# A hybrid decoder block: the attention head norm reads its PSUM bank, key transposes change banks, and the last head's output moves

## The chip, the cores and the metric

The kernel runs on one core of one Trainium2 chip, as one program. The metric is the device time of one execution in microseconds; the time of a kernel is the median of its runs. The profile is of one further execution, with the time of every instruction.

## What is computed

One decoder block on 512 tokens of width 1024, in float32. A normalised input is projected to queries, keys, values, and to the inputs of a state-space branch and of gates. Two branches run on it, differential attention (8 heads) and a Mamba-2 scan; each is projected, multiplied by sigmoid gates and added; an output projection, a residual and a gated MLP follow. The change touches the attention branch alone:

```python
q = rms_norm(q.reshape(b, s, ATTN_HEADS, 2, ATTN_HEAD_DIM), q_norm_g[l]) * scale
k = rms_norm(k.reshape(b, s, ATTN_HEADS, 2, ATTN_HEAD_DIM), k_norm_g[l])
...
p = jax.nn.softmax(logits, axis=-1)
a = p[:, :, 0] - lam * p[:, :, 1]
return jnp.einsum('bhqk,bhkv->bhqv', a.astype(v.dtype), v)
...
o = rms_norm(o, attn_subln_g[l], SUBLN_EPS) * (1.0 - lam_init)
y_attn = jnp.transpose(o, (0, 2, 1, 3)).reshape(b, s, V_COLS)
```

So each head gives 512 x 128 values `o`, and each row of `o` is scaled by the reciprocal root of its mean square: the head norm.

## The kernel before, in words

Every matrix product is made of three float32r matmuls (high part by high, high by low, low by high), so TensorE does most of the work. Weights arrive in tiles of 128 x 1024 on the SP queue and are split into `wh` (ScalarE, L83) and `wl` (VectorE, L85).

The order of the stages is: input norm, the state-space branch with its projections, attention, the merge of the branches (L775 to L787), the output projection, the MLP. The attention stage is one hand-written list of `pieces`, short runs of projection matmuls that keep TensorE busy: the query, key and value projections of four pairs of heads (`pair_pieces`, 24 pieces of 12 matmuls of 256 columns a pair), gate projections (`gate_pieces`), and at the end part of the projection of the attention output (`pa_pieces`, L709 to L723; the last three pieces have three matmuls each). Between pieces stand the steps of attention, hung on piece numbers by `put`. `steps[n]` is the piece behind which step n stands. With four query tiles of 128 tokens a head, step n does the logits of tile n (`logits`), the transposes of the probabilities of tile n - 2 (`flip_a`), the value matmuls of tile n - 3 (`values`), and in every fourth step `head_out` of a finished head. `prep(h)` transposes the queries and keys of head h five or six pieces ahead of its first logits, for the first head four ahead.

The framework orders each engine's instructions from this order of calls and from when it reckons their inputs to be ready, so an instruction can stand later than it is called. It adds the waits. An engine carries out its instructions in that order.

What the change touches:

- `prep` (L608 to L633): four transposes of queries into one `tp` bank and four of keys into another (L614). ScalarE copies the queries twice (L622, L623), VectorE takes their low part `ql` (L624); the keys are scaled (L629) and their low part taken (L630), `ks`. `tp` has two banks, which `flip_a` (L672) and `head_out` (L701) use as well. `mm`, with three banks, is that of the projections.
- Ahead of it, POOL scales the queries and then the keys of a pair (L586, `qk`).
- `values` (L676 to L696): the value matmuls of a tile go to columns of the one `po` bank (L682). After the fourth tile ScalarE copies the bank to `o` (L689) and squares the four tiles with a row sum each (L691). VectorE turns the sums into scales (L692, `rsqrt` at L113 to L122, L695), 13 small operations, and POOL multiplies `o` by them (L696).
- `head_out` (L698 to L705): four transposes of `o` (L701), then the high and low part `yaH`, `yaL` (L703, L704) for the output projection (L720 to L722, L779 to L781).
- The queue of steps (L744 to L767), where the last head's `head_out` comes behind all pieces.

Of the kernel before, what the change touches and what calls it, by code (L numbers as in the profile page):

```python
# [9 lines left out]
F32 = mybir.dt.float32  # L10
F32R = mybir.dt.float32r
I32 = mybir.dt.int32
AF = mybir.ActivationFunctionType
# [5 lines left out]
P = 128  # L19
S = 512  # L20
# [5 lines left out]
NH = 8  # L26
# [69 lines left out]
def block_kernel(ctx, tc, xt, ws, cols, heads, lams, relb, ident_d, ut_d, onehot_d, mline_d, out):  # L96
    nc = tc.nc
    V, A, G, T = nc.vector, nc.scalar, nc.gpsimd, nc.tensor

    const = ctx.enter_context(tc.tile_pool(name="const", bufs=1))  # L100
    small = ctx.enter_context(tc.tile_pool(name="small", bufs=4))
    dram = ctx.enter_context(tc.tile_pool(name="scratch", bufs=1, space=DRAM))
    mm = ctx.enter_context(tc.tile_pool(name="mm", bufs=3, space=PSUM))
    tpp = ctx.enter_context(tc.tile_pool(name="tpp", bufs=2, space=PSUM))
# [8 lines left out]
    def rsqrt(v, out_t, n, scale=None):  # L113
        it = small.tile([P, 32], I32, name="rsi", bufs=2)[:, :n]
        y = small.tile([P, 32], F32, name="rsy", bufs=2)[:, :n]
        t = small.tile([P, 32], F32, name="rst", bufs=4)[:, :n]
        V.tensor_scalar(out=it, in0=v.bitcast(I32), scalar1=1, scalar2=None, op0=ALU.logical_shift_right)
        V.tensor_scalar(out=y.bitcast(I32), in0=it, scalar1=-1, scalar2=0x5F3759DF, op0=ALU.mult, op1=ALU.add)
        for step in range(3):
            V.scalar_tensor_tensor(out=t, in0=y, scalar=-0.5, in1=y, op0=ALU.mult, op1=ALU.mult)  # L120
            V.tensor_mul(out=t, in0=t, in1=v)
            V.scalar_tensor_tensor(out=out_t if step == 2 else y, in0=t, scalar=1.5, in1=y, op0=ALU.add, op1=ALU.mult)  # L122
# [97 lines left out]
    with tc.tile_pool(name="dtp", bufs=1, side="right", reuse_waits="tile") as dp:  # L220
# [20 lines left out]
        for g in range(NG):  # L241
            nc.sync.dma_start(out=cum_d[g].rearrange("c h l -> h c l"),
                              in_=cum[g * HPG:(g + 1) * HPG, :].rearrange("h (c l) -> h c l", c=NCH))
# [7 lines left out]
        for i, src in enumerate((cum, wrow, dtr)):  # L251
            for c in range(NCH):
                o = (i * NCH + c) * 32
# [229 lines left out]
    for g, (dec0, xw0, chunks, last, norm) in enumerate(SSD_AT):  # L483
        def put(n, f, *a):
            at.setdefault(n, []).append(lambda: f(*a))
# [35 lines left out]
    ap = att_ctx.enter_context(tc.tile_pool(name="att", bufs=2, side="right", reuse_waits="tile"))  # L521
# [86 lines left out]
    def prep(h):  # L608
        st, hh, H = pairs[h // 2], h % 2, heads_[h]
        tps = []  # L610
        for nm in ("q", "k"):
            tp = tpp.tile([P, S], F32, name="tp")
            for t in range(4):
                T.transpose(out=tp[:, t * P:(t + 1) * P],  # L614
                            in_=st[nm][:, t, 2 * hh:2 * hh + 2, :].rearrange("p a d -> p (a d)"), identity=ident)
            tps.append(tp)
        tq, tk = tps
        H["q"], H["k"] = [], []
        for m in range(2):
            a, b = slice(m * 64, m * 64 + 64), slice(64 - m * 64, 128 - m * 64)  # L620
            q2 = ap.tile([P, S], F32R, name=f"qq{m}")
            A.copy(out=q2[a], in_=tq[a])  # L622
            A.copy(out=q2[b], in_=tq[a])  # L623
            V.tensor_sub(out=qlow[hh][m][a], in0=tq[a], in1=q2[a].bitcast(F32))  # L624
            H["q"].append(q2)
        for m in range(2):
            a, b = slice(m * 64, m * 64 + 64), slice(64 - m * 64, 128 - m * 64)
            k2 = ap.tile([P, S], F32R, name=f"ks{m}")
            A.activation(out=k2[a], in_=tk[a], func=AF.Copy, scale=gqk[a, 0:1])  # L629
            V.scalar_tensor_tensor(out=k2[b], in0=tk[a], scalar=gqk[a, 0:1], in1=k2[a].bitcast(F32),  # L630
                                   op0=ALU.mult, op1=ALU.subtract)
            H["k"].append(k2)
        H["r"] = small.tile([P, 4, 2], F32, name="es", bufs=3)  # L633
# [42 lines left out]
    def values(h, i):  # L676
        H, hh, vt = heads_[h], h % 2, pairs[h // 2]["v"]
        if i == 0:
            H["po"] = pop.tile([P, S], F32, name="po")
        po, aT = H["po"], H["aT", i]  # L680
        for b in range(i + 1):
            T.matmul(po[:, i * P:(i + 1) * P], lhsT=aT[:, b * P:(b + 1) * P], rhs=vt[:, b, hh * P:(hh + 1) * P],  # L682
                     start=(b == 0), stop=(b == i))
        if i < 3:
            return
        o = H["o"] = ap.tile([P, 4, P], F32, name="o")
        sq = ap.tile([P, P], F32, name="qksq", bufs=1)
        v = small.tile([P, 4], F32, name="ov", bufs=3)
        A.copy(out=o.rearrange("p a d -> p (a d)"), in_=po)  # L689
        for t in range(4):  # L690
            A.activation(out=sq, in_=o[:, t], func=AF.Square, scale=H["r"][:, t, 0:1], accum_out=v[:, t:t + 1])  # L691
        V.tensor_scalar(out=v, in0=v, scalar1=1.0 / P, scalar2=1e-5, op0=ALU.mult, op1=ALU.add)  # L692
        rr = small.tile([P, 4], F32, name="orr", bufs=2)
        rsqrt(v, rr, 4)
        V.scalar_tensor_tensor(out=rr, in0=rr, scalar=1.0 - LAM_INIT, in1=H["r"][:, :, 0], op0=ALU.mult, op1=ALU.mult)  # L695
        G.tensor_mul(out=o, in0=o, in1=rr.unsqueeze(2).to_broadcast([P, 4, P]))  # L696

    def head_out(h):  # L698
        tp = tpp.tile([P, S], F32, name="tp")
# [30 lines left out]
    pieces, start, todo = pair_pieces(0), [], {}  # L730
# [13 lines left out]
    steps = []  # L744
    for p_ in range(4):
        steps += [start[p_] + n for n in ((0, 3, 7, 10, 14, 17, 21, 24) if p_ < 2 else range(0, 24, 3))]
    steps += [steps[-1] + n for n in (3, 6, 9, 12, 15)]
    put(0, load_bias, 0)
    put(4, load_bias, 1)
    for h in range(NH):  # L750
        first = steps[4 * h] if h else start[0] + 1
        put(first - 6 if h % 2 else first - 5, prep, h)
    for n in range(4 * NH + 5):
        for f, back in ((logits, 0), (flip_a, 2), (values, 3)):
            if 0 <= n - back < 4 * NH:
                put(steps[n], f, (n - back) // 4, (n - back) % 4)
        if n % 4 == 3 and n // 4 + 2 < NH:
            put(steps[n], load_bias, n // 4 + 2)
        if n >= 8 and n % 4 == 0:
            put(steps[n], head_out, n // 4 - 2)  # L760
    for n, f in enumerate(pieces):
        f()
        for g in todo.pop(n, []):
            g()
# [35 lines left out]
    with tc.tile_pool(name="rsp", bufs=2, space=PSUM, reuse_waits="tile") as rsp, tc.tile_pool(name="wo", bufs=2, side="right", reuse_waits="tile") as op:  # L800
# [21 lines left out]
        first = []  # L822
# [136 lines left out]
```

## Time and profile before

| | |
|---|---|
| median of 3 runs | 1152.47 us (1152.27, 1152.47, 1157.36) |
| the profiled execution | 1156.34 us, span 1154.4 us |
| TensorE matmul | 1122.7 us busy, 97% of the span |
| VectorE | 760.8 us, 66% |
| ScalarE | 580.8 us, 50% |
| POOL | 121.7 us, 11% |
| granted TensorE clock | 0.995 of full speed over the span |

Times in the trace are microseconds from the start of the span. A wait is idle time of an engine ahead of an instruction, and the releaser named beside it is the instruction whose end it waited for. The attention stage lies between about 440 and 715 us. Matmuls overlap: each lasts longer than the distance to the next, so the rate of TensorE is read from starts.

### The profile page before, as it was taken

The page shows a single profiled execution, that of the slowest core. Times are in us where ns is not written, and L with a number is a line of the kernel's source. Part 1 is how long each engine was busy: PE and PEld are TensorE (multiplying, and loading weights), DVE is VectorE, ACT ScalarE, POOL GpSimd, SP SyncE. Part 2 cuts the span into 40 slices and gives each one's busy share as a digit, 9 for nine tenths or more (in the row PEclk, how much of TensorE's full clock was granted, in tenths as well). Part 3 has the DMA queues.
Part 4 walks back from the last instruction along what each step waited for, and adds up shares of the span by engine and source line. Part 5 has one row for each costly group of instructions (what it writes and reads, how often), then busy time and mean ns, then how long its engine had stood idle before and what let it go on. Part 6 is the DMA issues. An engine that isn't in the chain of part 4 may idle for free. (4 is left out here: it accounts for less than half of the span.)

```text
span 1154.4 us, 15737 instructions
## 1 busy us (share of the span) xinstructions
PE 1122.7 (97%) x5934; PEld 946.7 (82%) x5934; DVE 760.8 (66%) x1280; ACT 580.8 (50%) x1122; POOL 121.7 (11%) x157
## 2 busy tenths in 40 slices
PE   7999999999999999999999998999999999999998
PEld 4778788888887889998988887888888888888887
DVE  6858878669777574577778773646777777772220
ACT  5675665756664232567677663344444444441120
POOL 1002223111222200110101000021000000000000
PEclk9999999999999999999999998999999999999999
DMA  6462434333433223221212120353323333323320
GB/s 230 128 115 91 129 100 136 102 104 112 131 116 102 74 92 106 74 79 60 79 62 77 55 74 27 122 171 91 102 92 109 92 91 104 97 92 116 122 92 19
DMA packets 56556, 114.46 MB, mean 99 GB/s; under 512 B 20816, under 2 KB 28928, under 8 KB 56480
## 3 DMA queue, kind: packets, MB, share of 16 engines
q1 hardware_dynamic: 56336, 113.32, 31.9%
q8 instruction: 47, 0.77, 0.3%
q14 instruction: 29, 0.24, 0.1%
q10 hardware_dynamic: 144, 0.13, 0.0%
HBM read 111.19 MB, written 2.24 MB: 98 GB/s over the span
## 5 line engine op out<-in xcount | busy, mean ns | idle before, releaser
L83 ACT CAST wh<-wr 128x1024 fp32r<-128x1024 f32 x179 | 187.3, 1048 | 217.7 <-PE mm L205 172.9
L85 DVE TENSOR_TENSOR wl<-wr,wh 128x1024 fp32r<-128x1024 f32 x179 | 220.4, 1232 | 114.8 <-ACT wh L83 112.6
L204 PE MATMUL mm<-xH,wh 128*128 128x512 f32 x392 | 157.0, 400 | 8.4 <-ACT xH L176 7.1
L205 PE MATMUL mm<-xL,wh 128*128 128x512 f32 x392 | 155.4, 396 | 0.1
L206 PE MATMUL mm<-xH,wl 128*128 128x512 f32 x392 | 154.5, 394 | 0.0
L206 PE MATMUL mm<-hH,wl 128*128 128x512 f32 x352 | 137.2, 390 | 0.0
L204 PE MATMUL mm<-hH,wh 128*128 128x512 f32 x352 | 137.1, 390 | 0.0
L205 PE MATMUL mm<-hL,wh 128*128 128x512 f32 x352 | 137.1, 389 | 0.0
L538 PE MATMUL mm<-wh,xH 128*128 128x256 f32 x384 | 111.0, 289 | 0.0
L540 PE MATMUL mm<-wh,xL 128*128 128x256 f32 x384 | 109.0, 284 | 0.0
L539 PE MATMUL mm<-wl,xH 128*128 128x256 f32 x384 | 108.7, 283 | 0.0
L204 PEld LDWEIGHTS mm<-xH,wh 128*128 128x128 f32 x392 | 74.6, 190 | 26.6 <-ACT xH L176 7.8
L205 PEld LDWEIGHTS mm<-xL,wh 128*128 128x128 f32 x392 | 74.4, 190 | 16.7 <-DVE xL L177 2.1
L206 PEld LDWEIGHTS mm<-xH,wl 128*128 128x128 f32 x392 | 74.5, 190 | 15.2
L205 PEld LDWEIGHTS mm<-hL,wh 128*128 128x128 f32 x352 | 66.1, 188 | 13.8
L206 PEld LDWEIGHTS mm<-hH,wl 128*128 128x128 f32 x352 | 66.1, 188 | 13.7
L204 PEld LDWEIGHTS mm<-hH,wh 128*128 128x128 f32 x352 | 66.1, 188 | 13.5
L538 PEld LDWEIGHTS mm<-wh,xH 128*128 128x128 f32 x384 | 73.6, 192 | 0.2
L539 PEld LDWEIGHTS mm<-wl,xH 128*128 128x128 f32 x384 | 73.6, 192 | 0.2
L540 PEld LDWEIGHTS mm<-wh,xL 128*128 128x128 f32 x384 | 73.6, 192 | 0.0
L204 PE MATMUL mm<-aH,wh 128*128 128x512 f32 x176 | 68.5, 389 | 0.0
L206 PE MATMUL mm<-aH,wl 128*128 128x512 f32 x176 | 68.5, 389 | 0.0
(239 smaller groups left out, 2174.6 us busy)
## 6 DMA issues: line engine op xcount, KB each, us to landing
wr<-in_ws SPq DMA_DIRECT2D x179, 512.0 KB, 3.5
dec<-cum_d SPq DMA_DIRECT2D x16, 512.0 KB, 5.0
ec<-ecum_d SPq DMA_DIRECT2D x24, 128.0 KB, 4.9
xr<-in_xt SPq DMA_DIRECT2D x8, 256.0 KB, 2.7
out_y<-x SPq DMA_DIRECT2D x7, 256.0 KB, 2.0
x<-in_xt SPq DMA_DIRECT2D x3, 512.0 KB, 6.9
b<-line_d SPq DMA_DIRECT2D x8, 128.0 KB, 2.8
x<-in_xt SPq DMA_DIRECT2D x2, 256.0 KB, 5.2
```

The lines of the kernel that those rows point to most:

```text
L83: nc.scalar.copy(out=hi, in_=raw)
L85: nc.vector.tensor_sub(out=lo, in0=raw, in1=hi.bitcast(F32))
L204: T.matmul(ps, lhsT=h, rhs=rH(k), start=(k == 0), stop=False)
L205: T.matmul(ps, lhsT=h, rhs=rL(k), start=False, stop=False)
L206: T.matmul(ps, lhsT=l, rhs=rH(k), start=False, stop=(k == n - 1))
L538: T.matmul(ps, lhsT=xH[k][:, sl], rhs=h, start=(k == 0), stop=False)
L539: T.matmul(ps, lhsT=xH[k][:, sl], rhs=l, start=False, stop=False)
L540: T.matmul(ps, lhsT=xL[k][:, sl], rhs=h, start=False, stop=(k == NK - 1))
```

## The change

Three things are changed. In `prep` the key transposes go to a bank of `mm` in place of `tp`. In `values` a square with its row sum follows each query tile's value matmuls, straight from the `po` bank; the copy to `o` goes, and the final multiply is made by VectorE from `po`, in place of POOL from `o`. In the queue of steps the first two steps move back by two pieces and one, `prep` of the first head moves back by two pieces, and the last head's `head_out` moves from a step behind all pieces to the step before, which has two pieces behind it.

```diff
-            tp = tpp.tile([P, S], F32, name="tp")
+            tp = tpp.tile([P, S], F32, name="tp") if nm == "q" else mm.tile([P, S], F32, name="mm")
...
+        if i == 0:
+            H["ov"] = small.tile([P, 4], F32, name="ov", bufs=3)
+        v = H["ov"]
+        sq = ap.tile([P, P], F32, name="qksq", bufs=1)
+        A.activation(out=sq, in_=po[:, i * P:(i + 1) * P], func=AF.Square, scale=H["r"][:, i, 0:1], accum_out=v[:, i:i + 1])
         if i < 3:
             return
         o = H["o"] = ap.tile([P, 4, P], F32, name="o")
-        sq = ap.tile([P, P], F32, name="qksq", bufs=1)
-        v = small.tile([P, 4], F32, name="ov", bufs=3)
-        A.copy(out=o.rearrange("p a d -> p (a d)"), in_=po)
-        for t in range(4):
-            A.activation(out=sq, in_=o[:, t], func=AF.Square, scale=H["r"][:, t, 0:1], accum_out=v[:, t:t + 1])
...
-        G.tensor_mul(out=o, in0=o, in1=rr.unsqueeze(2).to_broadcast([P, 4, P]))
+        V.tensor_mul(out=o, in0=po.rearrange("p (a d) -> p a d", a=4), in1=rr.unsqueeze(2).to_broadcast([P, 4, P]))
...
-    steps += [steps[-1] + n for n in (3, 6, 9, 12, 15)]
+    steps[0] += 2
+    steps[1] += 1
+    steps += [steps[-1] + n for n in (3, 6, 9, 12)]
...
-        first = steps[4 * h] if h else start[0] + 1
-        put(first - 6 if h % 2 else first - 5, prep, h)
-    for n in range(4 * NH + 5):
+        put(steps[4 * h] - (6 if h % 2 else 5) if h else start[0] - 2, prep, h)
+    for n in range(4 * NH + 4):
...
+    put(steps[-1], head_out, NH - 1)
```

## Rows read from the trace of the kernel before

**Rows 1.** The page: busy us of each engine, share of the span, instructions.

```profile
PE 1122.7 (97%) x5934; PEld 946.7 (82%) x5934; DVE 760.8 (66%) x1280; ACT 580.8 (50%) x1122; POOL 121.7 (11%) x157
```

**Rows 2.** Waits of PE, 440 to 720 us: in total, times, longest.

```profile
PE tp L701 <- POOL o L696: 9.0, 7, 1.9
PE tp L614 <- POOL qk L586: 2.8, 3, 1.2
PE tp L672 <- DVE ql L624: 1.6, 5, 0.5
```

**Rows 3.** Timeline of PE, head 0: start, us, instruction [idle before <-releaser].

```profile
519.06 1.05 PE L682 MATMUL po<-vt,aT 128*128 128x128 f32 x8
...
525.99 0.38 PE L682 MATMUL po<-vt,aT 128*128 128x128 f32 x2
...
533.54 0.36 PE L538 MATMUL mm<-wh,xH 128*128 128x256 f32 x1
...
535.30 0.28 PE L540 MATMUL mm<-wh,xL 128*128 128x256 f32 x1
536.72 0.65 PE L701 MATMUL tp<-ident,o 128*128 128x128 f32 x4 [1.14 <-POOL o L696]
```

**Rows 4.** Timeline of ACT, head 0: the copy of the bank.

```profile
520.15 0.59 ACT L689 COPY o<-po 128x512 f32<-128x512 f32 x1 [0.57 <-PE po L682]
```

**Rows 5.** Timeline of DVE, 519 to 537 us.

```profile
521.90 0.17 DVE L662 RECIPROCAL es<-sums 128x2 f32<-128x2 f32 x1 [1.40 <-ACT p L660]
...
526.17 0.17 DVE L692 TENSOR_SCALAR ov<-ov 128x4 f32<-128x4 f32 x1
...
535.33 0.15 DVE L695 SCALAR_TENSOR_TENSOR orr<-orr,es 128x4 f32<-128x4 f32 x1
```

**Rows 6.** Timelines of ACT, DVE and POOL, the last head's norm.

```profile
705.95 0.59 ACT L689 COPY o<-po 128x512 f32<-128x512 f32 x1 [5.07 <-PE po L682]
...
708.46 0.19 ACT L691 ACTIVATION_READ_ACCUMULATOR qksq<-o,es 128x1 f32 x1
...
708.68 0.17 DVE L692 TENSOR_SCALAR ov<-ov 128x4 f32<-128x4 f32 x1 [10.37 <-ACT qksq L691]
...
711.14 0.16 DVE L695 SCALAR_TENSOR_TENSOR orr<-orr,es 128x4 f32<-128x4 f32 x1
...
711.47 1.04 POOL L696 TENSOR_TENSOR o<-o,orr 128x512 f32<-128x512 f32 x1 [15.38 <-DVE orr L695]
```

**Rows 7.** Timeline of PE at the end of the attention stage.

```profile
705.62 0.48 PE L720 MATMUL mm<-yaH,wh 128*128 128x512 f32 x1
...
710.25 0.39 PE L722 MATMUL mm<-yaH,wl 128*128 128x512 f32 x1
712.56 0.75 PE L701 MATMUL tp<-ident,o 128*128 128x128 f32 x4 [1.93 <-POOL o L696]
714.08 1.65 PE L779 MATMUL mm<-yaH,wh 128*128 128x512 f32 x3 [0.78 <-ACT yaH L703]
```

**Rows 8.** Windows: us, busy (x) PE PEld DVE ACT POOL, PEclk, DMA share, GB/s.

```profile
525.00:550.00 25.00, 23.63 (x177) 22.12 (x176) 18.41 (x46) 16.75 (x40) 1.45 (x2) 1.00 0.24 72
...
714.10:719.80 5.70, 5.70 (x14) 4.46 (x14) 3.73 (x5) 2.94 (x3) 0.00 (x0) 0.50 0.00 0
```

**Rows 9.** Groups by line, DVE, 480 to 712 us: busy, mean ns, idle before.

```profile
L558 DVE TENSOR_TENSOR gt<-mm,r_bc 128x512 f32<-128x512 f32 x8 | 5.5, 688 | 2.8 <-PE mm L556 2.8
```

**Rows 10.** Timelines of PE and POOL, the first head's transposes.

```profile
472.45 0.66 PE L614 MATMUL tp<-ident,qk 128*128 128x128 f32 x4 [0.56 <-POOL qk L586]
474.31 0.65 PE L614 MATMUL tp<-ident,qk 128*128 128x128 f32 x4 [1.20 <-POOL qk L586]
...
470.49 3.76 POOL L586 TENSOR_TENSOR qk<-qk,qkr 128x1024 f32<-128x1024 f32 x2 [21.83 <-PE mm L540]
```

**Rows 11.** Timelines of DVE and PE, head 5: last key read, next projection.

```profile
609.67 0.76 DVE L630 SCALAR_TENSOR_TENSOR ks<-tp,gqk,ks 64x512 fp32r<-64x512 f32 x1
...
610.69 0.36 PE L538 MATMUL mm<-wh,xH 128*128 128x256 f32 x1
```

## The prediction

> **What bounds the kernel now.** First the busy line of the page [rows 1]: TensorE (PE) is busy 97% of the span, VectorE (DVE) 66%, ScalarE (ACT) 50%, GpSimd (POOL) 11%. The change adds and removes no matmul, so all it can give back is time in which PE stands still or runs slowly. Second, the waits of PE in the attention stretch, 440 to 720 us [rows 2]: 9.0 us at L701, the transposes of a finished head, waiting for POOL's scaling at L696; 2.8 us at L614, the transposes of queries and keys; 1.6 us at L672, waiting for a PSUM bank that the query copies of `prep` still read. With the 0.78 us at the first L779 [rows 7] these 14.2 us, and what the clock does behind them, are the whole stake. The ends of matmuls are modelled, so a wait may cost some 0.1 us more than its row says.
>
> Third, why the head is late. The eight value matmuls of head 0 begin at 519.06 and last 1.05 us [rows 3]. ACT copies the bank at 520.15 [rows 4], but with other ACT work between its four squares the small rsqrt operations on DVE only begin at 526.17, and they run until 535.48 [rows 5], where the same 13 operations with DVE to themselves, in the last head, take from 708.68 to 711.30 [rows 6]. POOL scales for 1.04 us, and PE starts the transposes at 536.72 after 1.14 us of standing still [rows 3]. L701 is called directly behind the value matmuls of its step, yet 15 projection matmuls, issued from 533.54 to 535.30, stand between them on PE: the order of issue already allows for a late head, just not late enough.
>
> Fourth, the end of the stage, where nothing is left to fill PE [rows 6, 7]: last matmul of the pieces issued at 710.25, transposes at 712.56, first L779 at 714.08, and then matmuls that take twice their time. In 714.10 to 719.80 the granted clock is 0.50, that is 1.2 of 2.4 GHz, after PE had done only four transposes between 710.6 and 714.1 [rows 7, 8].
>
> **The change, part by part.**
>
> *Heads 0 to 6.* The copy of 128x512 (0.59 us, ACT) and the scaling on POOL (1.04 us) go; the four squares stay, but three run one, two and three steps earlier, each as its columns arrive. Behind the last value matmul stand one square, the 13 small DVE operations and a DVE multiply. A square costs (708.65 - 706.54) / 4 = 0.53 us with its accumulator read [rows 6]; from PSUM I take the same (0.2 us more or less would change nothing below). The multiply reads PSUM, as L558 does: 0.69 us [rows 9]. So head 0's chain begins at 520.11 + 0.04 + 0.53 = 520.7 instead of 526.2. Undisturbed it ends 2.62 + 0.69 us later, at 524.0; stretched to 9.3 us as now, at 530.7. Both lie before 535.4, where PE wants the result. The wait at L701 should vanish: 9.0 - 1.93 (last head) = **7.1 us** gained.
>
> What hides the new work: 8 x 0.69 = 5.5 us are added to DVE and 8 x 0.59 = 4.7 us taken from ACT over some 235 us; DVE waits between operations there (1.40 us at 521.90, just where the chain moves to [rows 5]). Without that cover the cost would be at most 5.5 us. Each early square waits on ACT for PE, with exponentials, copies and weight casts queued behind it; head 0's copy waited for PE in the same way and began 0.04 us after the last value matmul [rows 3, 4], so I take nothing for it. If the next value matmuls must wait for a square in the same bank, they have a step of 6.9 us (519.06 to 525.99) for 0.6 us of work.
>
> A sentence of the Trainium skill speaks against this part: VectorE: DVE Perf Modes, section "Rules for kernel authors", says to copy PSUM to SBUF first if many operations follow. The trace does not show that a copy would pay: the multiply that reads PSUM takes 0.69 us, and the copy alone 0.59 [rows 4, 9]; by the rule ACT would keep 4.7 us of copies, which PE does not see.
>
> *The wait that takes its place.* The single `po` bank was free when the copy ended, at 520.74. Now it is held until the multiply ends, and the next head's first value matmuls want it at 525.99 [rows 3]. Between 524.0 and 530.7 lies that time, so each of seven heads costs between nothing and 4.7 us. I take 0.3 us each, **-2 us**: the chain starts where DVE has gaps, and the issue order was seen above to push waiting PE work back, so only what it misjudges is lost.
>
> *Last head.* Square from 705.95 to 706.5, chain 2.62 us, multiply 0.69 us: ready at 709.8 instead of 712.51. `head_out` now stands behind piece 33, with two pieces, six matmuls, left. The 21 matmuls from 705.62 to 710.25 are (710.25 - 705.62) / 20 = 0.23 us apart [rows 7], so the first 15 end at 709.1; transposes from 709.85 to 710.5; six matmuls to 711.9, which cover the 0.69 us eviction; L779 at 711.9 instead of 714.08: **2.2 us**. PE then stands still 0.75 us at most, shorter than the 1.14 us at head 0, around which the granted clock stays at 1.00 [rows 8]. So the clock should stay up: 14 matmuls took 5.70 us instead of 14 x 0.23 = 3.2, **2.5 us** [rows 8]. The moved step issues four transposes, one ACT and one DVE operation, no DMA.
>
> *First head.* `prep(0)` stands two pieces later (2 x 12 matmuls of 256 columns, at (535.30 - 533.54) / 14 = 0.13 us [rows 3], some 3 us). Now its query transposes wait 0.56 us, its key transposes 1.20 us for POOL, which ends at 474.25 [rows 10]. With 3 us more work ahead of them both inputs are there: **1.8 us**. The logits of the first two tiles move back by two and one pieces, so `prep` keeps its lead; no DMA moves past another queue. The third L614 wait (2.8 - 1.8 = 1.0 us) stays.
>
> *Key transposes in a projection bank.* With the keys elsewhere a second `tp` bank is free for the transposes of probabilities: the 1.6 us of L672 [rows 2] should go, **1.6 us**. In return one of three `mm` banks is held until the last read of the keys. In the tightest place I found, in head 5, the keys are read until 610.43, and a projection starts at 610.69 [rows 11]: nearly even. Bounds 0 and 3 us for all heads; I take **-1 us**.
>
> *Sum.* 7.1 + 2.2 + 2.5 + 1.8 + 1.6 - 2 - 1 = 12.2 us against the profiled execution of 1156.34 us (span 1154.4): 1144.1. That execution lies 3.9 us above the median of 1152.47. Whether the median runs lost 2.5 us at the clock too is not shown; without it they gain 9.7 (1142.8), with it 12.2 (1140.3). I take **1142.0 us**.
>
> **The rivals.**
>
> *The stall only moves.* PE waits at L682 for the multiply instead of at L701 for POOL, about as long per head, and the 7.1 us are not gained: 1142 + 7 = 1149 us. For it: the chain's stretch on DVE, 9.3 against 2.6 us, is the same kind of misjudged lateness. Against it: the chain starts earlier. The Trainium skill, PSUM — Partial Sum Buffer, section "Summary: rules for kernel authors", says to evacuate PSUM promptly, and this change does the opposite; no row of before shows a PE wait on `po`. Chance 0.16.
>
> *The `po` bank becomes the bound (slower).* Place: L682 of the next head's first tile. It decides once the chain behind the last square takes over 525.99 - 520.7 - 0.69 = 4.6 us and PE's order is not pushed back. Price 4.7 us in seven heads, 33 us, against 14.2 gained: 1142 + 31 = 1173 us; half of it 1157 to 1158. For it: the chain takes 9.3 us now. Against it: those are 9.3 us amid the next head's query and key operations, and three squares no longer stand in front. Chance 0.06.
>
> *The heads stay late, or `mm` banks run short.* The multiply is placed so late on DVE that L701 still waits, or five heads each pay 1 to 2 us for a projection bank: 1147 to 1149 us. For it: head 5 above. Against it: 4.7 us between 530.7 and 535.4. Chance 0.14.
>
> **How the numbers follow.** The forecast has 0.64: 1137 (the new waits at zero, somewhat more than the rows at each stall) to 1146.7. Half a per cent of the median is 5.8 us, about what a measurement of this kernel can tell from no change, so faster is below 1146.7: 0.64 and a third of the 1147 to 1149 cases, 0.74. Within: 0.20. Slower: 0.06. The range from 1137 to 1150.5 leaves out the slow rival and a little at both ends.
>
> **What would show it.** Right: no L701 wait on POOL in heads 0 to 6; the small DVE chain beginning within about 1 us of the last value matmul; no stretch at granted clock 0.50 near 712; L614 waits down to about 1 us; L672 no longer waiting on `ql`. Wrong: waits of PE at L682 on the DVE multiply of more than 1 us a head, or of the projections (L538, L554) on `ks`, or PE's still time in 440 to 720 above 8 us.

## The result and the profile after

The changed kernel takes 1142.18 us in the median of four runs (1140.65 to 1143.94), the kernel before 1152.68 in the median of four beside it. The ratio is 0.990, with a 95% interval of 0.987 to 0.993: faster, 10.5 us, where 1142.0 was forecast. The profiled execution took 1140.65 us, span 1138.8 us.

The busy line of the page of the kernel after, which answers to [rows 1]:

```profile
PE 1116.3 (98%) x5934; PEld 943.0 (83%) x5934; DVE 766.3 (67%) x1288; ACT 574.6 (50%) x1114; POOL 110.0 (10%) x149
```

VectorE has 5.5 us more to do, ScalarE 6.2 and POOL 11.7 us less. Where the time came from is read stretch by stretch. In the windows below the columns are those of [rows 8]; the first stretch runs from the first query projection to the first matmul of the merge, the second to the last matmul of the merge. First the kernel before, then the kernel after:

```profile
441.50:714.10 272.60, 258.01 (x1873) 240.55 (x1871) 181.60 (x467) 167.16 (x409) 28.55 (x24) 1.00 0.22 69
714.10:745.50 31.40, 31.40 (x127) 25.71 (x128) 22.09 (x29) 11.46 (x14) 0.00 (x0) 0.91 0.34 106
```

```profile
439.20:700.80 261.60, 257.13 (x1872) 241.22 (x1871) 186.69 (x475) 160.94 (x401) 18.61 (x16) 1.00 0.24 72
700.80:729.60 28.80, 28.80 (x128) 23.52 (x127) 21.82 (x29) 11.45 (x14) 0.00 (x0) 1.00 0.36 116
```

The attention stage is 11.0 us shorter and the merge 2.6 us, the latter at a mean granted clock of 1.00 instead of 0.91. Another 2.3 us of the 15.6 us between these two spans lie ahead of the stage, where both kernels carry out the same instructions: there the profile of before shows a mean granted clock of 0.72 from 76 to 82 us and that of after 1.00. Seven of the twelve profiles taken in all have that stretch, four of them with the new head norm and three without, so it is not counted for the change. What it is worth of the 2.3 us is open: the stage begins between 439.4 and 441.5 us in the profiles with it and between 439.0 and 440.6 us in those without.

The waits of PE, 430 to 715 us, of the kernel after, against [rows 2]:

```profile
PE mm L614 <- POOL qk L586: 1.1, 1, 1.1
PE po L682 <- DVE o L696: 1.1, 4, 0.5
PE mm L538 <- ACT vt L591: 0.9, 1, 0.9
PE lg L649 <- ACT p L660: 0.8, 1, 0.8
PE tp L701 <- DVE o L696: 0.4, 1, 0.4
```

The 9.0 us at L701 have become 0.4, in the last head alone; L672 waits for nothing. What is new is small: 1.1 us for the `po` bank (the rows of the weight loads show more of it, see the last run below), 0.9 us of a projection that waits for a bank near 478 us, and 0.5 us more at the logits.

Head 0, timeline of DVE and then of PE, of the kernel after, against [rows 3, 5]:

```profile
516.67 0.17 DVE L692 TENSOR_SCALAR ov<-ov 128x4 f32<-128x4 f32 x1 [0.20 <-ACT qksq L688]
...
519.01 1.22 DVE L85 TENSOR_TENSOR wl<-wr,wh 128x1024 fp32r<-128x1024 f32 x1
...
520.41 1.23 DVE L85 TENSOR_TENSOR wl<-wr,wh 128x1024 fp32r<-128x1024 f32 x1
521.56 0.16 DVE L695 SCALAR_TENSOR_TENSOR orr<-orr,es 128x4 f32<-128x4 f32 x1
521.75 0.69 DVE L696 TENSOR_TENSOR o<-po,orr 128x512 f32<-128x512 f32 x1
```

```profile
515.03 1.05 PE L682 MATMUL po<-vt,aT 128*128 128x128 f32 x8
...
522.50 0.49 PE L682 MATMUL po<-vt,aT 128*128 128x128 f32 x2 [0.15 <-DVE o L696]
...
529.56 0.60 PE L701 MATMUL tp<-ident,o 128*128 128x128 f32 x4
```

The small chain begins 0.59 us after the last value matmul (516.08), not 6.1 us, and takes 5.05 us with two weight splits in between. The multiply ends at 522.44, and 0.06 us later the next head's first value matmuls enter the bank: they now follow the multiply closely. The head's transposes come 7.1 us after it and wait for nothing.

The end of the stage, timeline of PE of the kernel after, against [rows 7]:

```profile
694.15 1.05 PE L682 MATMUL po<-vt,aT 128*128 128x128 f32 x8
...
698.45 0.39 PE L720 MATMUL mm<-yaH,wh 128*128 128x512 f32 x1
699.20 0.63 PE L701 MATMUL tp<-ident,o 128*128 128x128 f32 x4 [0.36 <-DVE o L696]
...
700.83 0.86 PE L781 MATMUL mm<-yaH,wh 128*128 128x512 f32 x3
```

From the end of the last value matmuls to the first matmul of the merge 700.83 - 695.20 = 5.6 us pass. Before, those value matmuls stood at

```profile
704.81 1.05 PE L682 MATMUL po<-vt,aT 128*128 128x128 f32 x8
```

and it was 714.08 - 705.86 = 8.2 us.

### The profile page after: what moved, and what is told of

The parts are those of the page before. It is cut to its first block, busy times and chain, and to the rows that moved or that the text cites. A ratio compares the mean times of both kernels' runs of the same rounds, so it can differ in the third digit from the quotient of the medians.

```text
span 1138.8 us, 15720 instructions
## 1 busy us (share of the span) xinstructions
PE 1116.3 (98%) x5934; PEld 943.0 (83%) x5934; DVE 766.3 (67%) x1288; ACT 574.6 (50%) x1114; POOL 110.0 (10%) x149
## 4 chain that ended last, share of the span: by engine, by line
PE 86%; DVE 6%; ACT 3%; DMA 2%; issue 1%; SPq 1%; POOL 0%; DVEq 0%; ACTq 0%
PE mm L204 20%; PE mm L206 20%; PE mm L205 20%; PE mm L538 3%; PE mm L540 3%; PE mm L539 3%; DVE wl L85 1%; PE po L682 1%; PE sm L445 1%; ACT wh L83 1%; PE mm L555 1%; PE mm L554 1%; PE mm L556 1%; SPq L387 1%; PE sm L422 1%
## 5 line engine op out<-in xcount | busy, mean ns | idle before, releaser
L205 PE MATMUL mm<-aL,wh 128*128 128x512 f32 x176 | 68.5, 389 | 0.0
```

The source lines that it names most:

```text
L205: T.matmul(ps, lhsT=h, rhs=rL(k), start=False, stop=False)
```

## The experiments

The theory was the prediction's: late heads cost some 7 us at their transposes, the end of the stage the rest, and the parts add up. The first run repeats the kernel before, the next three are the parts alone.

**The kernel before once more**, unchanged, for the clock term.

> The kernel before, unchanged, profiled a second time. The profiled execution behind the prediction took 1156.34 us and showed the granted clock at 0.50 for about 7 us behind the last head and for about 3 us near 78 us. Theory A (the clock falls in nearly every execution of before): the new profile shows the stretch behind the last head again, and a time of 1152 to 1157. Rival B (the clock falls only in the slow-lying executions of before, so the median of 1152.7 never paid for it): a profile near 1152.5 us has no stretch at 0.50 between 700 and 720 us.

Ratio 1.000 (0.999 to 1.001). The windows of this second profile of before (the first two are stretches at the low clock, the last is the merge):

```profile
472.70:476.10 3.40, 3.40 (x16) 3.40 (x17) 1.78 (x3) 2.20 (x4) 0.00 (x0) 0.50 0.00 0
715.05:718.45 3.40, 3.40 (x10) 2.62 (x9) 2.62 (x4) 2.94 (x3) 0.00 (x0) 0.50 0.03 5
713.90:744.30 30.40, 30.39 (x126) 24.82 (x127) 22.11 (x29) 11.45 (x14) 0.00 (x0) 0.94 0.33 109
```

The clock falls behind the last head again, but for half as long, and the merge takes 30.4 us, 1.0 less than in the first profile and 1.6 more than after. Here it also falls behind the two waits at the first head's transposes. So Theory A holds for whether in the profiles, not for how much: the loss behind the last head is between 1.6 and 2.6 us in these two. In the profiles of the next kernels that keep the old norm the merge takes 30.1 and 30.3 us.

The mean granted clock, which is listed for every execution, says how common this is. Of 54 executions of the kernel before that were listed with it, 11 show 1.000; a stretch of 3.4 us at 0.50 alone would lower the mean to 0.9985 (an estimate from the windows above), so these 11 had none. Their median is 1151.88 us, that of all 54 is 1153.77, and that of the 11 at 0.995, like the profiled one, 1155.64. So "nearly every execution" was too strong. Rival B does not hold as it stands either: 27 of the 54 are at 0.997 or less, so the median pays for the clock somewhere in the span; where, the list does not say.

**The head norm alone.**

```diff
+        sq = ap.tile([P, P], F32, name="qksq", bufs=1)
+        A.activation(out=sq, in_=po[:, i * P:(i + 1) * P], func=AF.Square, ...)
         if i < 3:
             return
...
+        V.tensor_mul(out=o, in0=po.rearrange("p (a d) -> p a d", a=4), ...)
```

> Only the head norm is changed (squares per tile from PSUM, multiply on VectorE from PSUM). Theory A (the head norm is the main part, 7.1 us of waits at the heads' transposes plus most of the end of the stage): 1142 to 1146 us, no wait of PE at the heads' transposes in heads 0 to 6, waits on the po bank of about 1 us in all. Rival (the head norm only pays together with the free tp bank from the key transposes): 1149 to 1153 us.

1145.80 us, ratio 0.993 (0.992 to 0.994), 8.2 us of the runs' 1154.19. Its waits of PE, 430 to 730 us, and its clock at the end of the stage:

```profile
PE tp L614 <- POOL qk L586: 2.9, 3, 1.2
PE tp L672 <- DVE ql L624: 1.9, 3, 1.0
PE po L682 <- DVE o L696: 1.0, 3, 0.4
PE mm L779 <- ACT yaH L703: 0.8, 1, 0.8
PE lg L649 <- ACT p L660: 0.4, 1, 0.4
```

```profile
700.00:712.00 12.00, 11.22 (x50) 8.71 (x49) 8.30 (x21) 3.91 (x6) 0.00 (x0) 1.00 0.07 25
```

No head waits at L701, not even the last, and the clock stays at 1.00 although L779 still waits 0.8 us. The rival, that the norm needs the free bank, falls. The end of the stage on PE:

```profile
698.67 1.05 PE L682 MATMUL po<-vt,aT 128*128 128x128 f32 x8
...
705.72 0.97 PE L779 MATMUL mm<-yaH,wh 128*128 128x512 f32 x3 [0.78 <-ACT yaH L703]
```

From the end of the last value matmuls to the first matmul of the merge 6.0 us pass here, against 8.2 before.

**The key transposes alone.**

```diff
-            tp = tpp.tile([P, S], F32, name="tp")
+            tp = tpp.tile([P, S], F32, name="tp") if nm == "q" else mm.tile([P, S], F32, name="mm")
```

> Only the key transposes go to a projection bank. Theory A: the 1.6 us at the transposes of the probabilities go, about 1 us comes back as waits of projections for a bank: 1151.5 to 1153 us, no change that can be measured. Rival (the shared tp banks delayed whole steps): 1148 to 1150 us. Other rival (projections run short of banks): above 1155 us.

1153.61 us, ratio 1.000 (0.999 to 1.001): no change that can be measured. Its waits of PE, 430 to 730 us:

```profile
PE tp L701 <- POOL o L696: 9.9, 7, 1.9
...
PE lg L649 <- ACT p L660: 1.3, 2, 0.7
```

The 1.6 us at L672 are gone, but 0.9 us more stand at L701 and 1.0 us more at the logits. A theory of mine was wrong in the detail: what comes back is not a wait for a projection bank.

**The first head alone.**

```diff
+    steps[0] += 2
+    steps[1] += 1
...
-        first = steps[4 * h] if h else start[0] + 1
-        put(first - 6 if h % 2 else first - 5, prep, h)
+        put(steps[4 * h] - (6 if h % 2 else 5) if h else start[0] - 2, prep, h)
```

> Only the first head's transposes and the first two steps move back. Theory A: the two waits of 0.56 and 1.20 us at the first head's transposes go: 1150.5 to 1152 us. Rival (the logits of the first head then come late and give it back): 1152.5 us or more, with a new wait of PE before 500 us.

1151.26 us, ratio 0.998 (0.997 to 0.999), 2.4 us of 1154.19. Of its waits the row that mattered:

```profile
PE tp L614 <- POOL qk L586: 1.1, 1, 1.1
```

Of three waits at L614 (2.8 us) the one of head 6 is left, and nothing new stands before 500 us. The gain is a little over the 1.8 us of the two waits; the second profile of before shows the clock at 0.50 just behind them, which may be the rest.

The three parts sum to 8.2 + 0 + 2.4 = 10.6 us, and the whole gave 10.5 us, and 12.3 us in a second comparison (next but one). Within the intervals, some 3 us wide for each part, the parts add up.

**The last head's output, not moved.** Alone, on the kernel before, the moved step was not run. The last head's `o` is ready at 712.51 us there, after the last matmul of the pieces at 710.25 [rows 6, 7], so it should change nothing; that is argued and not shown. With the norm changed it moves four transposes by five matmuls:

```diff
-    steps += [steps[-1] + n for n in (3, 6, 9, 12)]
+    steps += [steps[-1] + n for n in (3, 6, 9, 12, 15)]
...
-    put(steps[-1], head_out, NH - 1)
```

> The changed kernel with the last head's output left behind all pieces, as before. On TensorE this moves four transposes five matmuls later and nothing else. Theory A (the early norm brings the end of the stage, the moved step only its last half microsecond): 0 to 1 us above the changed kernel, a wait of about 0.8 us at the merge's first matmul in place of the 0.36 us at the transposes, granted clock 1.00 throughout. Rival (the moved step is what keeps the clock up): a stretch at 0.50 near 702 us and 2 us or more above the changed kernel.

1141.88 us, ratio 0.990 (0.988 to 0.992), the same as the changed kernel. The wait at the merge and the clock there:

```profile
PE mm L781 <- ACT yaH L703: 0.8, 1, 0.8
```

```profile
698.00:710.00 12.00, 11.22 (x51) 8.75 (x50) 8.76 (x19) 4.29 (x6) 0.00 (x0) 1.00 0.20 66
```

The clock stays up without the moved step; the stage of this run is 262.0 us long against 261.6, in both profiles of the changed kernel. The moved step is worth these 0.4 us by the stage; the medians can't tell it from nothing.

**The changed kernel once more**, beside three variants of it on one chip.

> The changed kernel once more, beside the variants of it. Both theories: 0.988 to 0.992 of before; no stretch at granted clock 0.50 between 690 and 720 us.

1141.16 us, ratio 0.9895 (0.9875 to 0.9914). Its waits are those of the first profile but for the `po` bank, 0.8 us in two heads against 1.1 in four.

**Late squares: the rival of the `po` bank, made worse.**

```diff
-        if i == 0:
-            H["ov"] = small.tile([P, 4], F32, name="ov", bufs=3)
...
-        A.activation(out=sq, in_=po[:, i * P:(i + 1) * P], func=AF.Square, ...)
         if i < 3:
             return
+        v = small.tile([P, 4], F32, name="ov", bufs=3)
...
+        for t in range(4):
+            A.activation(out=sq, in_=po[:, t * P:(t + 1) * P], func=AF.Square, ...)
```

> The changed kernel, but with all four squares behind the last value matmul, from PSUM; the multiply stays on VectorE and the po bank is held some 5 us longer. Theory A (the issue order pushes the next head's value matmuls back, so a longer hold costs only what the order misjudges; what pays is the early start of the small chain): 1 to 5 us above the changed kernel, waits of PE on the po bank of under 1 us a head, and the last head's clock stretch comes back. Rival (the po bank bounds the heads): 14 us or more above the changed kernel, over 2 us of wait at each head's first value matmul.

1144.24 us, ratio 0.992 (0.990 to 0.993), 3.1 us above the changed kernel. Head 0 on DVE and PE, and the waits of PE, 430 to 730 us:

```profile
521.87 0.16 DVE L691 TENSOR_SCALAR ov<-ov 128x4 f32<-128x4 f32 x1
530.41 0.16 DVE L694 SCALAR_TENSOR_TENSOR orr<-orr,es 128x4 f32<-128x4 f32 x1
530.82 0.68 DVE L695 TENSOR_TENSOR o<-po,orr 128x512 f32<-128x512 f32 x1
```

```profile
531.55 0.94 PE L682 MATMUL po<-vt,aT 128*128 128x128 f32 x6 [0.81 <-DVE o L695]
```

```profile
PE po L682 <- DVE o L695: 3.4, 6, 0.8
PE lg L649 <- ACT p L660: 1.4, 2, 0.9
```

The bank is held 9 us longer than in the changed kernel (531.50 against 522.44), and yet the next head's first value matmuls wait 0.81 us: they stand so much later on PE, six in a row, the second tile behind the first. The bank as a bound falls, at 3.4 us where 14 or more were asked. One half of Theory A fell too: with waits of 0.6 and 0.8 us at the end of the stage the clock stayed at 1.00. And that the early start is what pays does not follow from this run: without it the kernel still gains 9.3 us of the 12.3 (some 2.4 of them in the first head), and only the last head waits at its transposes (0.6 us). Head 0's result comes 15.2 us behind its last value matmul, against 16.6 before and 6.4 in the changed kernel.

**Copy and POOL.** Early squares, but the bank is copied and POOL multiplies, as before.

```diff
+        A.copy(out=o.rearrange("p a d -> p (a d)"), in_=po)
...
-        V.tensor_mul(out=o, in0=po.rearrange("p (a d) -> p a d", a=4), ...)
+        G.tensor_mul(out=o, in0=o, ...)
```

> The changed kernel, but ScalarE copies the po bank to SBUF after the fourth square and POOL multiplies the copy, as before the change. Theory A (what pays is the early start, not the engine of the multiply): within 2 us of the changed kernel, no wait on the po bank, at most small waits at the heads' transposes. Rival (POOL's multiply was what made the heads late): the waits of 1.1 to 1.6 us at the heads' transposes are back, 6 to 8 us above the changed kernel.

1140.65 us, ratio 0.989 (0.987 to 0.991), not to be told from the changed kernel. Its wait at the heads' transposes, 430 to 730 us:

```profile
PE tp L702 <- POOL o L697: 2.8, 3, 1.1
```

Three heads wait, up to 1.1 us; four of the seven that waited before do not, though POOL multiplies all of them. No value matmul waits for the bank. So the early start is enough by itself. With the run before, where late squares and the multiply from the bank kept 9.3 us, this says that either half of the new norm takes most of the gain, and that both together take no more than the early start alone. Late squares with the copy kept and the multiply on VectorE were not run, so what in that other half pays, the copy that is gone or the engine, is not shown.

**The two waits that are left.** The first head's keys back in `tp`, head 6 one piece later.

```diff
-            tp = tpp.tile([P, S], F32, name="tp") if nm == "q" else mm.tile(...)
+            tp = tpp.tile([P, S], F32, name="tp") if nm == "q" or h == 0 else mm.tile(...)
...
-        put(steps[4 * h] - (6 if h % 2 else 5) if h else start[0] - 2, prep, h)
+        put(steps[4 * h] - (6 if h % 2 else 4 if h == 6 else 5) if h else start[0] - 2, prep, h)
```

> The changed kernel with two small moves: the first head's keys go back to a tp bank (against the 0.90 us wait of the projections for a bank near 478 us) and the transposes of head 6 come one piece later (against the 1.15 us wait for POOL near 626 us). Theory A (these two waits were real and independent): 1.5 to 2.5 us below the changed kernel. Rival (the waits only move to the logits of those heads): within 1 us of the changed kernel, with new waits of PE behind those places.

1139.21 us, ratio 0.988 (0.986 to 0.990), against 1141.16 and 0.9895 of the changed kernel; the intervals overlap, the stage is 260.1 us instead of 261.6. The 1.9 us between the medians lie where Theory A put them, but are not clear of noise. All waits of PE that are left, 430 to 730 us:

```profile
PE lg L649 <- ACT p L660: 1.3, 2, 0.8
PE po L682 <- DVE o L696: 0.8, 2, 0.5
PE tp L701 <- DVE o L696: 0.4, 1, 0.4
```

Both waits are gone, and the logits wait 0.5 us more.

**And the bank released early.** This version, with the copy on ScalarE and the multiply on VectorE.

```diff
+        A.copy(out=o.rearrange("p a d -> p (a d)"), in_=po)
...
-        V.tensor_mul(out=o, in0=po.rearrange("p (a d) -> p a d", a=4), ...)
+        V.tensor_mul(out=o, in0=o, ...)
```

> The version with the two moved key transposes, and besides it ScalarE copies the po bank behind the fourth square and VectorE multiplies the copy, so that the bank comes free without waiting for the small chain. Theory A (the waits on the bank, some 1.1 us in all, are all that the hold costs): 0 to 1.5 us below that version. Rival (the copy on ScalarE delays exponentials and evictions by as much): 0 to 1.5 us above it.

1136.69 us, ratio 0.985 (0.983 to 0.987): the fastest here, 4.5 us below the changed kernel, its interval just clear of that kernel's 0.9875 to 0.9914. The stage is 258.0 us. Its waits of PE, 430 to 730 us:

```profile
PE lg L649 <- ACT p L660: 1.2, 2, 0.6
PE tp L702 <- DVE o L697: 0.8, 2, 0.4
PE tp L702 <- DVE cf L664: 0.3, 1, 0.3
```

The step from the version before it is 2.1 us in the stage, by one profile of each, and 2.5 us in the medians, where the two intervals overlap; that is more than both theories allowed. The sums of PE's own waits, 2.5 and 2.3 us, differ by 0.2. The rest shows in the waits of the weight loads (PEld): a matmul's wait counts only from the modelled end of the matmul ahead of it. In the version before this one the loads for the value matmuls wait as follows, 430 to 730 us; here no such row is left:

```profile
PEld po L682 <- DVE o L696: 3.2, 7, 0.7
PEld po L682 <- ACT qksq L688: 0.5, 2, 0.3
```

All seven heads behind the first wait for the bank, 3.2 us in all, and two second tiles wait for the square of the tile ahead. Against these 3.7 us the heads' transposes wait 0.7 us more here (1.1 against 0.4). The difference of 3.0 us is the size of the gain and somewhat above it.

## Why the prediction was right

*Heads 0 to 6, 7.1 us.* Right in mechanism and size: no wait at L701 is left in them, and the norm alone gave 8.2 us with the end of the stage. Head 0's chain began at 516.67, 0.59 us behind the value matmuls, as worked out, and took 5.05 us, between the 2.6 and 9.3 of the bounds.

*The wait that takes its place, -2 us.* 1.1 us in PE's rows, in four heads. The reason that held was the one from [rows 3], that PE's order is pushed back: in the run with late squares the bank was held nine microseconds longer at head 0, and the wait for it was 0.8 us there and 3.4 us over six heads. Against an early release the hold costs 2.1 us in the stage, so the price taken, 0.3 us in each of seven heads, was right.

*Last head, 2.2 us.* 2.6 us. The sum took the early result and the moved step together and did not part them. The norm alone brings the 2.2 us (8.2 to 6.0 from the last value matmuls to the merge), and the moved step the last 0.4. Five matmuls stood behind the transposes, not the six of the sum.

*The clock, 2.5 us.* It stays up behind the last head in all eight profiles with the new norm or a variant of it, and fell in all four without (715, 711 and 710 us in the three taken later). The size was that of the first profile, 2.6 us by the merge; in the second 1.6, and 1.3 and 1.5 in the other two. Whether the median runs paid for the clock too was left open in the sum: they do somewhere in the span, though not in every execution, as the clocks of the 54 show. The 3.9 us by which the profiled execution lay above the median are about what parts the executions at 0.995 from those at 1.000. They are not the last head's stretch alone; there is the one near 78 us too, which the prediction did not look for.

*First head, 1.8 us.* The part alone gave 2.4 us, and both waits went.

*Key transposes, 1.6 against -1 us.* Alone the part gave nothing that can be measured, so the two nearly cancel. The gain was sized from a wait that did go; the cost came elsewhere, 0.9 us at L701 and 1.0 us at the logits when the part stood alone. With the other parts the bank cost 0.9 us, at 478 us in the first head, and not in head 5, which was named as the tightest place: there a projection did not wait. The look at one place did not find the worst one.

*The rivals.* The held bank as a bound, and the stall that only moves, both fell. So did the third, late heads or a lack of `mm` banks: no head but the last waits at L701, and one projection waits for a bank, 0.9 us. The Trainium skill, PSUM — Partial Sum Buffer, "Summary: rules for kernel authors", says to evacuate PSUM promptly. Here the trace agrees as far as a cost of 2.1 us goes; the gain did not end on it. The Trainium skill, VectorE: DVE Perf Modes, "Rules for kernel authors", offers a copy to SBUF first where many operations follow. The version with that copy is the fastest of those run. That the trace did not show the copy to pay, as the prediction had it, was right for ScalarE's time and wrong for the whole: it counted what the copy costs and not that it frees the bank.

*Luck.* That the median came out 0.2 us from the 1142.0 is luck in part. The four runs spread over 3.3 us, the choice between 1140.3 and 1142.8 was open, and the sum for the profiled execution, 12.2 us, stands against 13.6 in the stage and the merge of the two profiles.

## What to carry to other kernels

Where an engine waits for the end of a long chain of small operations, try both to start the chain earlier and to shorten its end, each alone: here three of four squares moved ahead brought as much as both together, with VectorE or with POOL for the multiply, and the shorter end alone most of it. A buffer held longer should be priced from the waits of the weight loads as well as of the matmuls. And a wait of TensorE is priced with what the clock does behind it, taken from more than one profile.

## What was not expected of the hardware

The granted clock fell to 0.50 for 6.8 us behind the last head in one profile of the kernel before and for 3.4 us in another, with the same waits of 1.93 and 0.78 us ahead of it. Behind the first head's waits of 0.56 and 1.20 us it fell in one of the four profiles that have them. The same order of instructions thus has executions that differ by some microseconds.
